# Squares of x: 64 products with ones on TensorE in place of 15 additions on VectorE

## The chip, the cores and the metric

One core of a Trainium2 chip runs the whole program. The metric is the time of one execution on the device in microseconds (us). The core's engines run side by side, each with its own queue in program order: TensorE (PE in the profile, its weight loads PEld), VectorE (DVE), ScalarE (ACT), GpSimd (POOL) and SyncE (SP), which issues the DMA transfers. They wait for one another by semaphores.

## The reference

Two layers of an encoder trunk over x, 512 positions of 2048 features, in float32. Each layer normalises x, scales and shifts it by values that come from a conditioning vector c, and mixes it. The start of it is what this case is about:

```python
def rms_norm(x, g):
    y = xf * lax.rsqrt(jnp.mean(xf * xf, axis=-1, keepdims=True) + EPS)
    return y * g

def ada_modulation(c, w_mod, b_mod):
    m = jax.nn.silu(c) @ w_mod + b_mod
    shift, scale, gate = jnp.split(m, 3, axis=-1)
    ...
for layer in range(DEPTH):
    shift, scale, gate = ada_modulation(c, w_mod[i], b_mod[i])
    h = rms_norm(x, norm_g[i]) * (1.0 + scale) + shift
    out = mixer(h, w_in[i], ..., w_out[i])
    x = x + gate * out
return rms_norm(x, final_norm_g)
```

The mixer of the first layer is an input projection 2048 to 8192 that feeds attention and a short convolution, and an output projection; that of the second is a gated unit with projections 2048 to 6144 and 2048 to 2048.

## The kernel before

x lies transposed: 16 tiles `x_t[kt]` of 128 features by 512 positions, loaded two tiles to a DMA, before everything else that is large. Since a position's features lie across partitions and across tiles, the mean of squares needs a sum over 16 tiles and then a sum over 128 partitions. The lines are those of the kernel before.

The head of the first layer goes like this. ScalarE squares the 16 tiles (L608). VectorE adds them up in two strands (L612) and the two strands together (L613, held as `total`). `inverse` (L201) sums over partitions: for each of four blocks of 128 positions one product with the block of squares as the stationary operand and one column of ones moving (L207), accumulated over the list of tiles that it is given; here that list has one tile. VectorE scales the four results into `r4` (L210, the tile is `r` in the profile), GpSimd raises them to -0.5 (L211). `rms` puts them on a diagonal (L218), `spread` multiplies that by ones (L224) and ScalarE copies the result to `r0` (L225), which holds the inverse root for each position on all partitions.

Beside this, `spread_cb` (L236) spreads silu(c) over all partitions into `cb` by 16 products (L241), whose results ScalarE and VectorE copy out. Conditioning is done on VectorE: `mod_tile` (L250) loads two halves of 128x1024 weights into `mraw` buffers and reduces each against `cb` with one instruction (L255, CUSTOM_DVE or ISA in the listings). In this stage there are five `mraw` buffers, and SyncE's queue waits at a load whose buffer has not been read.

The loop over the 16 tiles (L655) then does, per tile, two `mod_tile` (four halves: scale, then shift), `mod_scale` (L262), the loads of the projection weights and their split into a high and a low part (ScalarE L626, GpSimd L627), `modulated` (VectorE L562 into `tmp`, ScalarE L566 into `hh`, VectorE L569 into `lh`), and the products of the tile with the weights (L374 to L376). A scheduler sets the order on each engine from the order of the code and what depends on what; `tc.issue_after(total.ins)` tells it to place the first `mod_tile` of every round behind the last addition of squares.

The squares share their four group buffers (`hh`, four tiles each) with the high parts of the modulated tiles.

Of the kernel before, what the change touches and what calls it, by code (L numbers as in the profile page):

```python
# [11 lines left out]
AF = mybir.ActivationFunctionType  # L12
ALU = mybir.AluOpType
# [4 lines left out]
KT = D // P  # L18
# [97 lines left out]
def trunk(ctx, tc, xT, vecs, ab_wm, sg_wm, ab_wp, ab_wg, ab_wi, ab_wo, sg_wi, sg_wo, wsT, bs, rope, band, eye, out):  # L116
    nc = tc.nc
# [9 lines left out]
    def page(tag, bufs, dt=F32, pool=None):  # L127
        return (pool or work).tile([P, S], dt, tag=tag, bufs=bufs, name=tag)
# [44 lines left out]
    def bank():  # L173
        return psum.tile([P, S], F32, tag="ps", name="ps")
# [16 lines left out]
    x_t = Pages()  # L191
# [5 lines left out]
    def v1(c):  # L197
        return vec[:, c:c + 1]


    def inverse(parts, cols=ALL):  # L201
        n = (cols.stop - cols.start) // P
        sums = [bank() for _ in range(n)]
        for j, s in enumerate(parts):
            for i, acc in enumerate(sums):
                ts = slice(cols.start + i * P, cols.start + (i + 1) * P)
                nc.tensor.matmul(acc[:, 0:1], lhsT=s[:, ts], rhs=ones[:, 0:1], start=j == 0, stop=j == len(parts) - 1)  # L207
        r4 = const.tile([P, NT], F32, tag="r4", bufs=2, name="r4")
        for i, acc in enumerate(sums):
            nc.vector.tensor_scalar(out=r4[:, i:i + 1], in0=acc[:, 0:1], scalar1=1.0 / D, scalar2=EPS, op0=ALU.mult, op1=ALU.add)  # L210
        nc.gpsimd.tensor_tensor(out=r4[:, :n], in0=r4[:, :n], in1=mhalf[:, :n], op=ALU.pow)  # L211
        return r4

    def rms(parts, cols=ALL):
        r4, n = inverse(parts, cols), (cols.stop - cols.start) // P
        dg = page("tmp", 4)
        for i in range(n):
            nc.vector.tensor_scalar(out=dg[:, i * P:(i + 1) * P], in0=ident, scalar1=r4[:, i:i + 1], scalar2=None, op0=ALU.mult)  # L218
        return dg

    def spread(dg, r, cols=ALL):
        n = cols.stop - cols.start
        pr = bank()
        nc.tensor.matmul(pr[:, :n], lhsT=ones, rhs=dg[:, :n], start=True, stop=True)  # L224
        nc.scalar.copy(out=r[:, cols], in_=pr[:, :n])  # L225
# [24 lines left out]
    def mod_tile(pool, n, nt, bufs):  # L250
        src, b = wm[n]
        for h in range(2):
            raw = pool.tile([P, HALF], F32, tag="mraw", bufs=bufs, name="mraw")
            nc.sync.dma_start(out=raw, in_=src[nt, h])
            nc.vector.tensor_tensor_reduce(  # L255
                out=raw, in0=raw, in1=cb[:, h * HALF:(h + 1) * HALF], scale=0.5,
                scalar=v1(b + nt) if h == 0 else macc[n][:, nt:nt + 1], op0=ALU.mult, op1=ALU.add,
                accum_out=(mods if h else macc)[n][:, nt:nt + 1])

    def mod_scale(n, kt):  # L260
        g = v1((V_ABG if n == "ab" else V_SGG) + kt)
        nc.vector.scalar_tensor_tensor(  # L262
            out=gsc[n][:, kt:kt + 1], in0=mods[n][:, KT + kt:KT + kt + 1], scalar=1.0, in1=g,
            op0=ALU.add, op1=ALU.mult)
# [106 lines left out]
    def mm3(acc, w, m, first, last, **kw):  # L371


        nc.tensor.matmul(acc, lhsT=w[0], rhs=m[0], start=first, stop=False, **kw)  # L374
        nc.tensor.matmul(acc, lhsT=w[0], rhs=m[1], start=False, stop=False, **kw)  # L375
        nc.tensor.matmul(acc, lhsT=w[1], rhs=m[0], start=False, stop=last, **kw)  # L376

    class Pos:
# [3 lines left out]
        def slice(self):  # L382
            w = self.s.next(self.i, self.more)
            self.i += 1
            if self.tick:
                self.tick(self.s.last.ins)
            return w
# [171 lines left out]
    def modulated(n, kt, t, r, to, cols=ALL, keep=False):  # L559

        xr = page("tmp", 4)
        nc.vector.scalar_tensor_tensor(  # L562
            out=xr[:, cols], in0=t[:, cols], scalar=gsc[n][:, kt:kt + 1], in1=r[:, cols], op0=ALU.mult, op1=ALU.mult)
        hi, lo = to
        sh = mods[n][:, kt:kt + 1]
        nc.scalar.activation(out=hi[:, cols], in_=xr[:, cols], func=AF.Identity, bias=sh)  # L566
        if keep:
            nc.scalar.activation(out=t[:, cols], in_=xr[:, cols], func=AF.Identity, bias=sh)
        nc.vector.scalar_tensor_tensor(  # L569
            out=lo[:, cols], in0=xr[:, cols], scalar=sh, in1=hi[:, cols].bitcast(F32), op0=ALU.add, op1=ALU.subtract)  # L570
# [32 lines left out]
    pa = tc.alloc_tile_pool(name="pa", bufs=2, reuse_waits="tile")  # L603
    parts = []
    squares = Book("hh", F32)
    for kt in range(KT):
        sq = squares.page()
        nc.scalar.activation(out=sq, in_=x_t[kt], func=AF.Square)  # L608
        if kt < 2:
            parts.append(sq)  # L610
        else:
            nc.vector.tensor_tensor(out=parts[kt % 2], in0=parts[kt % 2], in1=sq, op=ALU.add)  # L612
    total = nc.vector.tensor_tensor(out=parts[0], in0=parts[0], in1=parts[1], op=ALU.add)  # L613
    r0 = page("R", 2)
    spread(rms(parts[:1]), r0)

# [1 line left out]
    def split_w(src, n, pool, bufs):  # L620
        raw = work.tile([P, HALF], F32, tag="wraw", bufs=3, name="wraw")[:, :n]
        size = HALF if pool is work else n
        hi = pool.tile([P, size], F32R, tag="whi", bufs=bufs, name="whi")[:, :n]
        lo = pool.tile([P, size], F32R, tag="wlo", bufs=bufs, name="wlo")[:, :n]
        nc.sync.dma_start(out=raw, in_=src)
        nc.scalar.copy(out=hi, in_=raw)  # L626
        nc.gpsimd.tensor_tensor(out=lo, in0=raw, in1=hi.bitcast(F32), op=ALU.subtract)  # L627
        return hi, lo
# [4 lines left out]
    def fetch(g, kts):  # L633
        for kt in kts:
            held[g, kt] = split_w(ab_wg[g, kt], S, pa, 8)

    def quarter(g, q):
        if q == 0:
            sums[g] = pa.tile([P, 4, S], F32, tag="sum", bufs=1, name="sum") if g == 1 else work.tile([P, 4, S], F32, tag="xy", bufs=4, name="xy")
        for f in range(4):  # L640
            acc = bank()
            cs = slice(f * P, (f + 1) * P)
            for i in range(4):
                kt = 4 * q + i
                (hi, lo), a = held[g, kt], h[kt]
                if g:
                    mm3(acc, (hi[:, cs], lo[:, cs]), a, i == 0, i == 3)
                else:
                    mm3(acc, (a[0][:, cs], a[1][:, cs]), (hi, lo), i == 0, i == 3)
            if q == 0:  # L650
                nc.scalar.copy(out=sums[g][:, f], in_=acc)
            else:
                nc.vector.tensor_tensor(out=sums[g][:, f], in0=acc, in1=sums[g][:, f], op=ALU.add)

    for kt in range(KT):  # L655
        with tc.issue_after(total.ins):
            mod_tile(pa, "ab", KT + kt, 5)
        mod_scale("ab", kt)
        mod_tile(pa, "ab", kt, 5)
        hi, lo = split_w(ab_wp[kt], W_P, work, 2)  # L660
        modulated("ab", kt, x_t[kt], r0, h.add())
        for f in range(6):
            cs = slice(f * P, (f + 1) * P)
            mm3(gates[f], (hi[:, cs], lo[:, cs]), h[kt], kt == 0, kt == KT - 1)
        fetch(0, [kt])
        q, i = divmod(kt, 4)
        if q:
            at = 4 * (q - 1) + 2 * (i % 2)
            fetch(1 + i // 2, [at, at + 1])
            if i % 2:  # L670
                quarter(1 + i // 2, q - 1)
        if i == 3:
            quarter(0, q)
# [211 lines left out]
    parts = right()  # L885
# [134 lines left out]
    parts = right()  # L1020
# [7 lines left out]
    for i in range(2):  # L1028
        for g in range(4):
# [5 lines left out]
            if g % 2:  # L1035
                (nc.scalar if g > 1 else nc.sync).dma_start(
                    out=out[1].rearrange("(t p n) -> t p n", t=2, p=P)[i, :, (g - 1) * S:(g + 1) * S].rearrange("p (g s) -> p g s", g=2),
                    in_=fin[i][:, g - 1:g + 1])
# [84 lines left out]
```

## Time and profile before

| | us |
|---|---|
| median of three runs | 1690.81 (1689.48 to 1692.96) |
| the profiled execution | 1690.71 |
| its span, first to last instruction | 1688.6 |
| TensorE busy | 1614.2 (96%) |
| VectorE busy | 1309.0 (78%) |
| ScalarE busy | 664.6 (39%) |
| GpSimd busy | 143.4 (8%) |

The shares are averages over the span. The chain that ended last, followed back from the end, is 80% TensorE and 13% VectorE. The page's 40 slices are 42 us each, with the busy share in tenths. The granted clock of TensorE is 1.00 at full speed (2.4 GHz) and 0.50 at its lower level (1.2 GHz).

### The profile page before, as it was taken

The numbers are of one execution on the slowest core, as the hardware profiler recorded it, in microseconds if no ns is written. First come the engines' busy times: TensorE is split into PE (matmuls) and PEld (weight loads), VectorE is DVE, ScalarE is ACT, GpSimd is POOL, SyncE is SP. The second block draws the span as 40 slices with busy tenths as digits, with TensorE's granted clock in tenths as the row PEclk, the third lists the DMA queues.
The fourth block names the chain that finished last, engine by engine and source line by source line (L and its number), as shares of the span: only waits on it lengthen the run. The fifth ranks groups of instructions, "written<-read, shape, count | busy, mean of one in ns | idle before, by whom it ended". The sixth has DMA issues, their size and how long they took to land.

```text
span 1688.6 us, 24674 instructions
## 1 busy us (share of the span) xinstructions
PE 1614.2 (96%) x9900; PEld 1440.9 (85%) x9900; DVE 1309.0 (78%) x1761; ACT 664.6 (39%) x953; POOL 143.4 (8%) x95
## 2 busy tenths in 40 slices
PE   5888999999999999999999999699999999999998
PEld 3676787888888888888889998699999999998998
DVE  7899748876766777766878876788998888898884
ACT  3232224332322332323544554344444444465552
POOL 2465521000000000000000000000000000000000
PEclk7999999999999999999999999799999999999999
DMA  8787544765666665764453432233333333235333
GB/s 312 255 278 261 193 129 144 225 227 193 225 210 232 216 224 182 247 210 164 135 190 125 152 130 69 75 101 101 100 101 101 103 100 118 97 101 199 109 99 115
DMA packets 85539, 276.44 MB, mean 164 GB/s; under 512 B 8753, under 2 KB 11057, under 8 KB 85425
## 3 DMA queue, kind: packets, MB, share of 16 engines
q1 hardware_dynamic: 85136, 273.82, 48.5%
q8 instruction: 77, 1.26, 0.3%
q10 hardware_dynamic: 288, 1.05, 0.2%
q14 instruction: 38, 0.30, 0.1%
HBM read 266.45 MB, written 8.39 MB: 163 GB/s over the span
## 4 chain that ended last, share of the span: by engine, by line
PE 80%; DVE 13%; issue 3%; ACT 2%; DMA 1%; SPq 0%; POOL 0%; POOLq 0%; DVEq 0%; ACTq 0%
PE ps L376 26%; PE ps L374 26%; PE ps L375 26%; DVE mraw L255 5%; DVE wlo L310 2%; ACT whi L309 1%; PE ps L974 1%; PE ps L735 1%; DVE gsc_ab L262 1%; DMA xy<-in_xT_dram 1%; DVE st L953 1%; DVE first L434 0%; ACT hh L566 0%; DVE lh L569 0%; DVE third L310 0%
## 5 line engine op out<-in xcount | busy, mean ns | idle before, releaser
L374 PE MATMUL ps<-hh,whi 128*128 128x512 f32 (+1 forms) x1600 | 568.3, 358 | 22.1 <-ACT hh L566 16.1
L376 PE MATMUL ps<-hh,wlo 128*128 128x512 f32 (+1 forms) x1600 | 566.5, 354 | 1.3 <-POOL wlo L627 1.3
L375 PE MATMUL ps<-lh,whi 128*128 128x512 f32 (+1 forms) x1600 | 566.3, 354 | 1.5 <-DVE lh L797 1.5
L374 PEld LDWEIGHTS ps<-hh,whi 128*128 128x128 f32 x1600 | 304.0, 190 | 68.8 <-ACT hh L566 19.8
L309 ACT CAST whi<-wraw 128x1024 fp32r<-128x1024 f32 x190 | 199.7, 1052 | 406.4 <-PE ps L375 294.2
L376 PEld LDWEIGHTS ps<-hh,wlo 128*128 128x128 f32 x1600 | 303.3, 190 | 44.1 <-POOL wlo L627 2.1
L375 PEld LDWEIGHTS ps<-lh,whi 128*128 128x128 f32 x1600 | 303.7, 190 | 43.5 <-DVE lh L797 1.9
L310 DVE TENSOR_TENSOR wlo<-wraw,whi 128x1024 fp32r<-128x1024 f32 x190 | 232.7, 1226 | 121.6 <-ACT whi L309 120.9
L255 DVE CUSTOM_DVE_ANT_0 mraw<-mraw,cb,vec 128x1024 f32<-128x1024 f32 x96 | 138.5, 1443 | 18.2 <-DMA mraw<-in_sg_wm_dram 12.9
L627 POOL TENSOR_TENSOR wlo<-wraw,whi 128x512 fp32r<-128x512 f32 (+1 forms) x64 | 114.9, 1814 | 105.8 <-ACT whi L626 93.0
L374 PE MATMUL ps<-whi,hh 128*128 128x512 f32 (+1 forms) x288 | 103.9, 361 | 19.5 <-ACT whi L309 15.1
L376 PE MATMUL ps<-sum,wlo 128*128 128x256 f32 x408 | 113.0, 277 | 0.9 <-DVE wlo L310 0.9
L374 PE MATMUL ps<-sum,whi 128*128 128x256 f32 x408 | 112.7, 276 | 0.0
L375 PE MATMUL ps<-sum,whi 128*128 128x256 f32 x408 | 112.7, 276 | 0.0
L309 ACT CAST whi<-first 128x1024 fp32r<-128x1024 f32 x56 | 58.8, 1050 | 116.4 <-DVE first L318 69.2
L375 PE MATMUL ps<-wlo,hh 128*128 128x512 f32 (+1 forms) x288 | 103.0, 358 | 0.8 <-DVE wlo L310 0.7
L376 PE MATMUL ps<-whi,lh 128*128 128x512 f32 (+1 forms) x288 | 102.8, 357 | 0.0
L310 DVE TENSOR_TENSOR wlo<-first,whi 128x1024 fp32r<-128x1024 f32 x56 | 68.4, 1222 | 26.2 <-ACT whi L309 26.2
L255 DVE CUSTOM_DVE_ANT_0 mraw<-mraw,cb,macc_ab 128x1024 f32<-128x1024 f32 x48 | 79.6, 1657 | 1.6 <-DMA mraw<-in_ab_wm_dram 0.5
L374 PEld LDWEIGHTS ps<-whi,hh 128*128 128x128 f32 x288 | 55.4, 192 | 29.5 <-ACT whi L309 15.5
L376 PEld LDWEIGHTS ps<-sum,wlo 128*128 128x128 f32 x408 | 76.6, 188 | 1.4 <-DVE wlo L310 1.4
L318 DVE TENSOR_TENSOR first<-first,wraw 128x1024 f32<-128x1024 f32 x63 | 76.8, 1219 | 0.5
(253 smaller groups left out, 2884.3 us busy)
## 6 DMA issues: line engine op xcount, KB each, us to landing
mraw<-in_ab_wm_dram SPq DMA_DIRECT2D x96, 512.0 KB, 4.6
mraw<-in_sg_wm_dram SPq DMA_DIRECT2D x96, 512.0 KB, 4.5
wraw<-in_ab_wi_dram SPq DMA_DIRECT2D x92, 512.0 KB, 3.6
wraw<-in_sg_wi_dram SPq DMA_DIRECT2D x75, 512.0 KB, 3.5
wraw<-in_ab_wo_dram SPq DMA_DIRECT2D x27, 512.0 KB, 3.5
wraw<-in_sg_wo_dram SPq DMA_DIRECT2D x27, 512.0 KB, 3.5
wraw<-in_ab_wg_dram SPq DMA_DIRECT2D x48, 256.0 KB, 2.8
first<-in_sg_wi_dram SPq DMA_DIRECT2D x21, 512.0 KB, 3.8
```

Of the source, the lines that this page charges most:

```text
L255: nc.vector.tensor_tensor_reduce(out=raw, in0=raw, in1=cb[:, h * HALF:(h + 1) * HALF], scale=0.5, scalar=v1(b + nt) if h == 0 else macc[n] ...
L262: nc.vector.scalar_tensor_tensor(out=gsc[n][:, kt:kt + 1], in0=mods[n][:, KT + kt:KT + kt + 1], scalar=1.0, in1=g, op0=ALU.add, op1=ALU.mult)
L309: nc.scalar.copy(out=hi, in_=raw)
L310: nc.vector.tensor_tensor(out=lo, in0=raw, in1=hi.bitcast(F32), op=ALU.subtract)
L318: nc.vector.tensor_tensor(out=r[a], in0=r[a], in1=r[b], op=ALU.add)
L374: nc.tensor.matmul(acc, lhsT=w[0], rhs=m[0], start=first, stop=False, **kw)
L375: nc.tensor.matmul(acc, lhsT=w[0], rhs=m[1], start=False, stop=False, **kw)
L376: nc.tensor.matmul(acc, lhsT=w[1], rhs=m[0], start=False, stop=last, **kw)
L627: nc.gpsimd.tensor_tensor(out=lo, in0=raw, in1=hi.bitcast(F32), op=ALU.subtract)
L735: nc.tensor.transpose(out=pt[:, i * P:(i + 1) * P], in_=ps[i][:, ks], identity=ident)
L953: nc.vector.bn_stats(out=st[:, j, n, :], in_=t)
L974: nc.tensor.matmul(accs[f][:, j * P:(j + 1) * P], lhsT=y.g[n][:, j, f * P:(f + 1) * P], rhs=wst[g // 4][:, g % 4 * P:(g % 4 + 1) * P], sta ...
```

## The change

All 16 squares are kept and handed to `rms`, so that the products with ones sum over tiles and partitions at once: 16 tiles by 4 blocks. Every fourth square is taken on VectorE instead of ScalarE. The additions go, and with them `total` and the `issue_after` that used it.

```diff
     for kt in range(KT):
         sq = squares.page()
-        nc.scalar.activation(out=sq, in_=x_t[kt], func=AF.Square)
-        if kt < 2:
-            parts.append(sq)
+        if kt % 4 == 3:
+            nc.vector.tensor_tensor(out=sq, in0=x_t[kt], in1=x_t[kt], op=ALU.mult)
         else:
-            nc.vector.tensor_tensor(out=parts[kt % 2], in0=parts[kt % 2], in1=sq, op=ALU.add)
-    total = nc.vector.tensor_tensor(out=parts[0], in0=parts[0], in1=parts[1], op=ALU.add)
+            nc.scalar.activation(out=sq, in_=x_t[kt], func=AF.Square)
+        parts.append(sq)
     r0 = page("R", 2)
-    spread(rms(parts[:1]), r0)
+    spread(rms(parts), r0)
...
     for kt in range(KT):
-        with tc.issue_after(total.ins):
-            mod_tile(pa, "ab", KT + kt, 5)
+        mod_tile(pa, "ab", KT + kt, 5)
         mod_scale("ab", kt)
```

The code above is what is written; the scheduler decides where each instruction stands. On VectorE, from the sum of squares to the first modulation of x (L562), the rows before are:

```order
L612 TENSOR_TENSOR hh<-hh 128x512 x10
L613 TENSOR_TENSOR hh<-hh 128x512
L255 ISA mraw,macc_ab<-mraw,cb,vec 128x1024
L255 ISA macc_ab 128x1
L210 TENSOR_SCALAR r_172<-ps 128x1 x4
L255 ISA mraw,mod_ab<-mraw,cb,macc_ab 128x1024
L255 ISA mod_ab 128x1
L218 TENSOR_SCALAR tmp<-ident,r_172 128x128 x4
L262 SCALAR_TENSOR_TENSOR gsc_ab<-mod_ab,vec 128x1
L255 ISA mraw,macc_ab<-mraw,cb,vec 128x1024
```

The same place in the changed kernel, whose line numbers are three smaller for the squares and up to two smaller further down:

```order
L609 TENSOR_TENSOR hh<-xy 128x512 x2
L210 TENSOR_SCALAR r_217<-ps 128x1 x4
L218 TENSOR_SCALAR tmp<-ident,r_217 128x128 x4
L255 ISA mraw,macc_ab<-mraw,cb,vec 128x1024
L255 ISA macc_ab 128x1
L255 ISA mraw,mod_ab<-mraw,cb,macc_ab 128x1024
L255 ISA mod_ab 128x1
L262 SCALAR_TENSOR_TENSOR gsc_ab<-mod_ab,vec 128x1
L255 ISA mraw,macc_ab<-mraw,cb,vec 128x1024
L255 ISA macc_ab 128x1
L562 SCALAR_TENSOR_TENSOR tmp<-xy,gsc_ab,R 128x512
```

The first two reductions (the rows with `cb`), which stood around the four `r` operations, stand behind the four of the diagonal. From the fourth reduction on the two orders run alike again.

On TensorE, before, from the products that spread silu(c) to the first products with weights:

```order
L241 MATMUL ps<-ident,cs 128x128 x16
L207 MATMUL ps<-ones,hh 128x1 x4
L224 MATMUL ps<-tmp,ones 128x512
L374 MATMUL ps<-hh,whi 128x512 x6
L374 MATMUL ps<-whi,hh 128x512
```

And in the changed kernel:

```order
L241 MATMUL ps<-ident,cs 128x128 x16
L207 MATMUL ps<-ones,hh 128x1 x64
L224 MATMUL ps<-tmp,ones 128x512
L374 MATMUL ps<-hh,whi 128x512
L375 MATMUL ps<-lh,whi 128x512
L376 MATMUL ps<-hh,wlo 128x512
```

Four products with ones have become 64, in the same place in the queue, in groups of four in the order of the tiles, each group waiting for its square.

## Rows read from the trace of the kernel before

**Rows 1.** The page's 40 slices: busy tenths of TensorE and VectorE.

```profile
PE   5888999999999999999999999699999999999998
DVE  7899748876766777766878876788998888898884
```

**Rows 2.** Busy time by stretch: us, busy time and count of each engine, granted clock.

```profile
core 0: us, PE busy (x) PEld busy (x) DVE busy (x) ACT busy (x) POOL busy (x), PEclk, DMA share, GB/s
9.30:11.00 1.70, 0.00 (x0) 0.00 (x0) 1.70 (x4) 1.70 (x4) 0.00 (x0) 1.00 1.06 412
11.00:11.50 0.50, 0.00 (x0) 0.00 (x0) 0.50 (x2) 0.50 (x2) 0.00 (x0) 0.81 1.02 393
...
18.60:20.60 2.00, 1.86 (x8) 1.78 (x8) 1.54 (x6) 0.00 (x0) 0.00 (x0) 0.50 1.04 415
...
28.40:184.00 155.60, 130.75 (x528) 102.19 (x528) 143.66 (x164) 43.90 (x70) 86.98 (x46) 0.96 0.76 264
184.00:260.00 76.00, 75.86 (x334) 62.63 (x335) 35.07 (x49) 21.04 (x33) 28.15 (x20) 1.00 0.43 139
```

**Rows 3.** Chain of waits, first 330 us: start, length, what ran.

```profile
14.77 1.16 ACT hh L608 x2
...
17.91 0.70 DVE hh L613
18.65 1.88 PE ps L207 x8
20.87 1.98 POOL r L211
...
23.89 2.06 PE ps L224 x2
...
26.59 0.75 DVE tmp L562
...
45.31 1.28 DVE mraw L255
46.64 1.28 DVE mraw L255
```

**Rows 4.** VectorE's waits, 28 to 185 us: total, times, longest.

```profile
DVE lh L569 <- ACT hh L566: 9.0, 12, 1.5
```

**Rows 5.** L612 and L608: ns min/median/max, first and last start, shapes.

```profile
L612 DVE TENSOR_TENSOR hh<-hh x14: 681/684/693, 7.8 to 17.2; 128x512 f32<-128x512 f32 x14
...
L608 ACT ACTIVATE hh<-xy x16: 612/621/635, 5.8 to 15.3; 128x512 f32<-128x512 f32 x16
```

**Rows 6.** L207, the products with ones, in the first 40 us.

```profile
L207 PE MATMUL ps<-ones,hh x8: 352/352/370, 18.7 to 20.2; 128*128 128x1 f32 x8
```

**Rows 7.** Weight loads in order of time around 980 us: start, length, instruction.

```profile
979.91 0.54 PEld L207 LDWEIGHTS ps<-ones,R 128*128 128x128 f32 x4
980.36 0.53 PEld L207 LDWEIGHTS ps<-ones,tmp 128*128 128x128 f32 x4
980.81 0.19 PEld L374 LDWEIGHTS ps<-hh,whi 128*128 128x128 f32 x1
```

**Rows 8.** L241, the products that spread silu(c).

```profile
L241 PE MATMUL ps<-ident,cs x32: 275/421/581, 3.2 to 9.0; 128*128 128x128 f32 x32
```

**Rows 9.** VectorE in order of time, 15 to 31 us.

```profile
18.52 1.28 DVE L255 CUSTOM_DVE_ANT_0 mraw<-mraw,cb,vec 128x1024 f32<-128x1024 f32 x1
...
20.68 1.28 DVE L255 CUSTOM_DVE_ANT_0 mraw<-mraw,cb,macc_ab 128x1024 f32<-128x1024 f32 x1
...
22.87 0.88 DVE L218 TENSOR_SCALAR tmp<-ident,r 128x128 f32<-128x128 f32 x4 [0.90 <-POOL r L211]
...
26.59 0.75 DVE L562 SCALAR_TENSOR_TENSOR tmp<-xy,gsc_ab,R 128x512 f32<-128x512 f32 x1 [0.25 <-ACT R L225]
```

**Rows 10.** VectorE's reductions by operands, 28 to 185 us: busy us, mean ns.

```profile
L255 DVE CUSTOM_DVE_ANT_0 mraw<-mraw,cb,macc_ab 128x1024 f32<-128x1024 f32 x28 | 52.6, 1879 | 0.8
L255 DVE CUSTOM_DVE_ANT_0 mraw<-mraw,cb,vec 128x1024 f32<-128x1024 f32 x28 | 47.8, 1705 | 1.3 <-DMA mraw<-in_ab_wm_dram 1.3
```

## The prediction

> **What bounds the kernel now.** I read the page's 40 slices first [rows 1]. TensorE is at 9 tenths or more from the fifth slice on; only the first four slices (42 us each) fall short, and there VectorE is at 7 to 9. A table by stretches sharpens this [rows 2]: from 28.4 to 184.0 us VectorE works 143.66 of 155.6 us, TensorE 130.75; from 184 to 260 TensorE works 75.86 of 76. So there are two regimes: a first stage paced by VectorE, then a stage paced by TensorE to the end. The change lies wholly at the head of the first stage.
>
> The chain of waits [rows 3] shows that head step by step. The last tiles of x are there at 14.77; ScalarE squares them until 15.9; VectorE's additions lag and end at 18.61 (17.91 + 0.70); four small products take 1.88 us; then come the power on GpSimd (1.98), the diagonal, the spreading product (2.06), the copy to r0 and at 26.59 the first modulation of x (L562). From there the chain is mostly conditioning reductions (L255) at a period of 1.33 us (46.64 - 45.31). In this stage VectorE waits little: 9.0 us, in 12 waits, for the ScalarE half of the modulation [rows 4]. A delay of VectorE's work at the head therefore finds no slack to vanish in: every later step of the stage hangs on it, and TensorE's stage behind that.
>
> **The change part by part.**
> *VectorE's work on squares.* Out go 15 additions of 0.684 us (10.3 us) [rows 5]; in come 4 squarings, a tensor_tensor on the same 128x512 shape, which I price alike (2.7 us). ScalarE loses 4 squares of 0.62 us. Neither is bounding any more: the last square, on VectorE, can start when x lands at 14.77 and ends near 15.5, against 18.61 for the sum now. If nothing else changed, that alone would be worth 3.1 us.
>
> *The products.* 4 become 64, each with a 128x128 block of squares as the stationary operand and one moving column. The row of L207 shows two passes per product (x8 for 4 products) [rows 6]. Cold, eight passes took 1.86 us, the last lasting about 0.36, so they start (1.86 - 0.36) / 7 = 0.214 us apart. Late in the kernel, where the clock is granted in full, the weight loads of eight such passes run from 979.91 to 980.81, 0.1125 us each [rows 7]. So 128 passes cost 14.3 us at the high clock (2.4 GHz) and 27.3 us at the low one (1.2 GHz). They are on the path: TensorE runs in order, and they stand behind the 32 passes of L241, whose last starts at 9.0 [rows 8]. A tile of x comes every 0.64 us (16 squares start between 5.8 and 15.3 [rows 5]), but four products need 0.9 us at best. TensorE is behind from its first product on and no longer waits for x.
>
> The Trainium skill, "TensorE: Matmul & The Clock Gate", section "LDWEIGHTS (loading the stationary operand)", prices a weight load by its columns alone, 128 / 1.2 = 107 ns: as an estimate, 128 loads would be 13.7 us at either clock. The rows agree at the high clock (0.1125) and not at the low one (0.214).
>
> *Which clock.* After L241 the granted clock stayed at 1.00 to 11.0 us, averaged 0.81 from 11.0 to 11.5 and was 0.50 by the time L207 ran [rows 2]: a mean of 0.81 is 0.31 us of the half microsecond at full clock, so it fell at 11.31, 2 us after TensorE's last pass. Now TensorE does not idle there, but what it does is load weights for single columns. No row shows a long run of that. Bounds: all at the high clock, the first pass starts one spacing after L241's last, at 9.11, and the last at 9.11 + 127 x 0.1125 = 23.4; falling at 11.31 as now, 2.20 / 0.1125 = 19.5 passes are done by then and 107.5 x 0.214 = 23.0 us follow, last start 34.3. Today's last pass starts at 18.65 + 1.50 = 20.15. The delay is 3.25 us by the first and 14.15 by the second. I take the second: the nearest row is L207's own, in the same place after the same L241, and it ran at 0.50 through all its passes.
>
> *Conditioning.* The issue_after goes, but the order on VectorE shows that the reductions do not come earlier. Now one pair of them runs between the sum and the diagonal, while TensorE and GpSimd work (18.52 and 20.68 [rows 9]); in the changed order both stand behind the four r4 operations (which wait for the last product) and the four of the diagonal (which wait for GpSimd). VectorE then idles from 15.5 until the last product, and its first reduction starts only after the diagonal. That moves two reductions out of cover: 2 x 1.33 = 2.66 us. The modulation waited 0.25 us for r0 [rows 9]; with two reductions more in front of it that wait is gone, so 2.4 us net. Queued behind the waiting r4 operations is everything VectorE does for the stage, and SP too: the reductions free the five mraw buffers, so loads beyond the fifth wait as well. That costs nothing of its own, because five tiles are there when VectorE starts, and it frees one per 1.33 us while it still has four to read.
>
> *After the head.* On SP and GpSimd the order of instructions stays as it was; ScalarE and TensorE differ beyond the squares only in a few rows of the first modulated tile, which wait for the same events. I price that at nothing, with an uncertainty: with GpSimd running, L255 averages 1.88 and 1.71 us over the stage [rows 10] instead of 1.28 [rows 9], 56 x 0.5 = 28 us in all. How the two engines mesh after a shifted start may move that by a tenth, 3 us either way.
>
> Sum: 14.15 + 2.4 = 16.55 us. The profiled execution took 1690.71 us (span 1688.6 and 2.1 around it), 0.1 below the median of the three runs, 1690.81. Forecast: 1690.7 + 16.6 = 1707.3 us, 1704 to 1711 on its own with the 3 us above.
>
> **Rivals.**
> 1. *The clock stays up.* A TensorE that is never idle keeps its 2.4 GHz through all 64 products. For it: the clock fell only after idling here. Against it: L207 ran wholly at 0.50. Time: 3.25 + 2.4 = 5.65 us, 1696.4 us (1693.4 to 1699.4). The Trainium skill, same page, section "What's actually happening", has the gate follow how busy the engine is; taken by its word, this rival would be the outcome. No run so far shows what a stream of one-column products counts for.
> 2. *Not slower: the products keep pace with x.* If weight loads slipped under one another, the products would follow each square, and the last pass would start near 15.6, just after the last square. The sum would be ready 4.5 us earlier than today, conditioning would give back 2.4, and the time would be 1690.7 - 2.1 = 1688.6 us. It decides from the point at which a product costs under 0.16 us (0.64 / 4); the cheapest pair of passes in the trace is 0.225. The Trainium skill, same page, section "Step-by-step: what each phase is for", speaks for it: the engine pulls the next load ahead of a running matmul. The rows already contain whatever of that happens.
> 3. *The change does not do what it says.* "Not queued behind" already fails in the order; that is in the sum. Were conditioning the part that counts and the products nearly free, it would be rival 2.
> 4. *Worse than forecast.* The clock falls at once and VectorE meshes badly with GpSimd: 27.3 us of products from 9.11, so 16.2 + 2.4 + 3 = 21.6, 1712 us.
>
> **How the numbers follow.** Forecast 0.57, rival 1 0.32, rival 2 (with 3) 0.07, rival 4 0.04. 0.2% is 3.4 us, about what a measurement of this kernel can tell from no change. Slower by more than that (over 1694.2) are the forecast, rival 4 and 0.27 of rival 1, whose low end lies under it: 0.88. Same gets the other 0.05 of rival 1 and 0.04 of rival 2, faster the remaining 0.03 of rival 2: 0.09 and 0.03. The range spans rival 1 and the forecast and leaves out rivals 2 and 4: 1693.5 to 1711; the forecast's own is 1704 to 1711.
>
> **What would show it.** In the changed profile, L207 should have 128 passes from about 9.1 with no gap, the last starting near 34 (forecast) or 23 (rival 1); the spacing changes from 0.11 to 0.21 where the granted clock goes to 0.50, near 11.3. VectorE should idle from about 15.5 until then, and its first L255 should follow the four L218. The diagonal now ends at 23.75 (22.87 + 0.88 [rows 9]); three reductions stand between it and L562, which should first start near 23.75 + 14.15 + 3 x 1.33 = 41.9 (forecast) or 31.0 (rival 1) instead of 26.59, and the stretch in which TensorE takes over should begin as much after 184 as the total grew. I am wrong if L207 ends before 20 us, if L255 runs before L210, or if the delay at L562 shrinks on the way to 184, which would mean slack in the first stage that I did not see.

## The result and the profile after

The changed kernel takes 1703.95 us (median of four runs, 1703.22 to 1705.17) against 1691.15 us before: a ratio of 1.0083 with a 95% interval of 1.0070 to 1.0096, 12.8 us or 0.8% slower. The profiled execution took 1703.22 us, its span is 1701.2.

The slices of the page show where: only the first one changes much. TensorE has 7 tenths there instead of 5, VectorE 3 instead of 7 [rows 1].

```profile
PE   7889899999999999999999999699999999999998
DVE  3889837867766767676878876688998888898884
```

By stretches (us, busy time and count of each engine, granted clock, share of the DMA engines, GB/s), to be held against [rows 2]:

```profile
core 0: us, PE busy (x) PEld busy (x) DVE busy (x) ACT busy (x) POOL busy (x), PEclk, DMA share, GB/s
9.30:11.00 1.70, 1.70 (x19) 1.70 (x17) 1.29 (x2) 1.33 (x3) 0.00 (x0) 1.00 1.05 407
11.00:11.50 0.50, 0.50 (x6) 0.50 (x7) 0.00 (x0) 0.50 (x2) 0.00 (x0) 1.00 1.07 410
11.50:15.00 3.50, 3.50 (x32) 3.50 (x31) 1.18 (x2) 2.57 (x5) 0.00 (x0) 0.95 1.06 417
15.00:18.00 3.00, 3.00 (x16) 3.00 (x16) 0.21 (x1) 0.15 (x1) 0.00 (x0) 0.50 1.03 418
24.00:27.00 3.00, 3.00 (x15) 3.00 (x16) 0.00 (x0) 0.00 (x0) 0.00 (x0) 0.50 0.00 0
```

TensorE works without a gap, and its clock falls all the same. A mean of 0.95 over 3.5 us is 3.15 us at full speed and the rest at half: it fell near 14.65, not at 11.31. In the stretch from 24 to 27 TensorE is the only thing that moves: VectorE has nothing it may do, and not a byte is loaded. The products as one group (ns min/median/max, first and last start), beside [rows 6]:

```profile
L207 PE MATMUL ps<-ones,hh x128: 169/352/353, 9.1 to 31.1; 128*128 128x1 f32 x128
```

128 passes, the last starting at 31.1, 10.95 us after the last one of before (20.15). VectorE in order of time, beside [rows 9]:

```profile
14.52 0.69 DVE L609 TENSOR_TENSOR hh<-xy 128x512 f32<-128x512 f32 x1 [1.83 <-DMA xy<-in_xT_dram]
30.19 0.16 DVE L210 TENSOR_SCALAR r<-ps 128x1 f32<-128x1 f32 x1 [14.98 <-PE ps L207]
...
32.83 0.87 DVE L218 TENSOR_SCALAR tmp<-ident,r 128x128 f32<-128x128 f32 x4 [1.20 <-POOL r L211]
33.62 1.28 DVE L255 CUSTOM_DVE_ANT_0 mraw<-mraw,cb,vec 128x1024 f32<-128x1024 f32 x1
...
35.04 1.28 DVE L255 CUSTOM_DVE_ANT_0 mraw<-mraw,cb,macc_ab 128x1024 f32<-128x1024 f32 x1
...
37.65 2.28 DVE L562 SCALAR_TENSOR_TENSOR tmp<-xy,gsc_ab,R 128x512 f32<-128x512 f32 x1
```

The row to read is the second: 14.98 us in which VectorE, the engine that paces this stage, waits for TensorE. Its first reduction comes at 33.62 instead of 18.52. SyncE waits with it: four loads of conditioning weights take 24.83 us to issue (11.86 in the kernel before; rows of SyncE's queue in order of time, the first before, the second after), because their buffers are not read.

```profile
13.51 11.86 SPq L254 DMA_DIRECT2D mraw<-in_ab_wm_dram  x4
```

```profile
13.26 24.83 SPq L254 DMA_DIRECT2D mraw<-in_ab_wm_dram  x4
```

Then the delay travels. The two reductions that the chain of waits had at 45.31 and 46.64 [rows 3] now stand here:

```profile
58.77 1.28 DVE mraw L255
60.09 1.28 DVE mraw L255
```

That is 13.46 us later. The first modulations of the 16 tiles, L562 as a group, run from 26.6 to 192.5 us before (first row) and from 37.6 to 205.2 after:

```profile
L562 DVE SCALAR_TENSOR_TENSOR tmp<-xy,gsc_ab,R x16: 741/752/1751, 26.6 to 192.5; 128x512 f32<-128x512 f32 x16
```

```profile
L562 DVE SCALAR_TENSOR_TENSOR tmp<-xy,gsc_ab,R x16: 750/752/2280, 37.6 to 205.2; 128x512 f32<-128x512 f32 x16
```

The last one is 12.7 us late, and the span is 12.6 us longer. Of 13.5 us at the head 0.8 were given back along the stage, none after it. In a second profile of the changed kernel (run 6) the third tile is as late and the last L562 starts at 204.0, so there 2.0 us were given back. What follows the stage hardly varies: in nine of the eleven profiles of this case the span ends 1495.8 to 1496.6 us after the start of the last L562 (1498.7 and 1498.2 in runs 3 and 8). How late the stage ends is, but for those two, what the kernel loses.

### The profile page after: what moved, and what is told of

It reads as the page before. It is cut to its first block, busy times and chain, and to the rows that moved or that the text cites. A ratio compares the mean times of both kernels' runs of the same rounds, so it can differ in the third digit from the quotient of the medians.

```text
span 1701.2 us, 24889 instructions
## 1 busy us (share of the span) xinstructions
PE 1636.1 (96%) x10020; PEld 1462.2 (86%) x10020; DVE 1299.7 (76%) x1750; ACT 663.5 (39%) x949; POOL 143.1 (8%) x95
## 4 chain that ended last, share of the span: by engine, by line
PE 79%; DVE 13%; issue 2%; ACT 2%; DMA 1%; DVEq 0%; POOLq 0%; ACTq 0%; SPq 0%
PE ps L376 26%; PE ps L374 26%; PE ps L375 26%; DVE mraw L255 4%; DVE wlo L310 2%; DMA mraw<-in_ab_wm_dram 1%; PE ps L972 1%; ACT whi L309 1%; PE ps L733 1%; DVE gsc_ab L262 1%; DVE tmp L562 1%; DVE st L951 1%; DVE first L434 0%; DVE third L310 0%; ACT hh L566 0%
## 5 line engine op out<-in xcount | busy, mean ns | idle before, releaser
L255 DVE CUSTOM_DVE_ANT_0 mraw<-mraw,cb,vec 128x1024 f32<-128x1024 f32 x96 | 137.6, 1434 | 22.9 <-DMA mraw<-in_sg_wm_dram 16.3
L310 DVE TENSOR_TENSOR wlo<-first,whi 128x1024 fp32r<-128x1024 f32 x56 | 68.4, 1222 | 26.6 <-ACT whi L309 26.6
L255 DVE CUSTOM_DVE_ANT_0 mraw<-mraw,cb,macc_ab 128x1024 f32<-128x1024 f32 x48 | 75.0, 1563 | 2.5 <-DMA mraw<-in_ab_wm_dram 1.5
```

What stands on the lines that cost most here:

```text
L255: nc.vector.tensor_tensor_reduce(out=raw, in0=raw, in1=cb[:, h * HALF:(h + 1) * HALF], scale=0.5, scalar=v1(b + nt) if h == 0 else macc[n] ...
L310: nc.vector.tensor_tensor(out=lo, in0=raw, in1=hi.bitcast(F32), op=ALU.subtract)
```

## The experiments

Each is compared with runs of the kernel before on the same chip; ratios are to those. "Reductions" are the conditioning instructions of L255, whose line moves by one to three in the variants. Eight kernels beside the changed one were run, in three sets.

**1. The order alone: reductions behind the diagonal, with the additions and 4 products of before.**

`last[0]` is the last instruction of the diagonal, kept by `rms`; the scale's `mod_tile` stands behind `total` already.

```diff
     spread(rms(parts[:1]), r0)
+    total = last[0]
...
-        mod_tile(pa, "ab", kt, 5)
+        with tc.issue_after(total.ins):
+            mod_tile(pa, "ab", kt, 5)
```

> The kernel before, with its additions and its 4 products, in which the scheduler is told to place the conditioning reductions behind the diagonal (L218), where the changed kernel has them. Theory A (two separate costs: the 64 products delay the sum of squares by 11 us, and two reductions moved out of the products' cover cost 2.4 us more): 1691.2 + 2.4 = 1693.6 us, with L562 first starting near 29.1 instead of 26.59. Rival B (the place of the reductions costs nothing, all of it is the products): 1691.2 us, within 0.05%.

Measured: ratio 1.0014 (1.0006 to 1.0023), 2.4 us on 1689.7, with an interval from 1.0 to 3.9. Its VectorE in order of time:

```profile
20.05 0.16 DVE L210 TENSOR_SCALAR r<-ps 128x1 f32<-128x1 f32 x1 [0.27 <-PE ps L207]
21.41 0.88 DVE L220 TENSOR_SCALAR tmp<-ident,r 128x128 f32<-128x128 f32 x4 [1.20 <-POOL r L211]
22.20 1.28 DVE L257 CUSTOM_DVE_ANT_0 mraw<-mraw,cb,vec 128x1024 f32<-128x1024 f32 x1
...
28.90 1.63 DVE L564 SCALAR_TENSOR_TENSOR tmp<-xy,gsc_ab,R 128x512 f32<-128x512 f32 x1
...
45.37 0.75 DVE L564 SCALAR_TENSOR_TENSOR tmp<-xy,gsc_ab,R 128x512 f32<-128x512 f32 x1
```

The first reduction comes at 22.20 instead of 18.52, the modulation at 28.90, near the expected 29.1. By the time, the place of the reductions has a price of its own, the smaller part of the 12.8 us; rival B, within 0.05%, lies just outside the interval.

The trace does not show that price at the head. The diagonal starts 1.46 us sooner than before (21.41 against 22.87), because the additions end 0.5 us sooner and GpSimd's power takes 1.02 us instead of 1.98. Four reductions then stand in a row, where the changed kernel has three. By the third tile (45.37, the last row) the modulation is only 0.73 us later than in the kernel before:

```profile
44.64 0.75 DVE L562 SCALAR_TENSOR_TENSOR tmp<-xy,gsc_ab,R 128x512 f32<-128x512 f32 x1
```

At the last tile it is 3.2 us later (195.7 against 192.5), in an execution that is the slowest of the eleven (1693.6). So 2.4 us is the price of this order as a whole; that it is the lost cover of two reductions is not shown.

**2. Two reductions ahead of the r4 operations in the changed kernel.**

```diff
-    spread(rms(parts), r0)
+    early = [mod_tile(pa, "ab", nt, 5) for nt in (KT, 0, KT + 1, 1)[:1]]
+    spread(rms(parts, behind=early[-1].ins), r0)
...
```

`behind` makes the r4 operations follow the last of the early reductions, and the loop leaves out what is already there.

> The changed kernel, in which the first two reductions are placed ahead of the r4 operations, under the products. Theory A: 1704.0 - 2.7 = 1701.3 us; the products still end near 31 and L562 starts near 36, when r0 is there. Rival B: unchanged, 1704 us. Rival C (the price is VectorE's idle time, not the lateness of r0): also 2.7 us less, so this run does not part A and C.

Measured: ratio 1.0079 (1.0062 to 1.0097), 1702.85 us, with runs from 1698.6 to 1707.2. That does not part 1701.3 from 1704. The profiled run shows a new loss: the diagonal took 3.43 us instead of 0.87, beside GpSimd. It does not explain why the median is no lower, for this execution is the fastest of the six (1698.6), and in it the third tile is modulated 3.8 us sooner than in the changed kernel (54.27 against 58.10). Why the six spread so far stays open.

```profile
33.66 3.43 DVE L219 TENSOR_SCALAR tmp<-ident,r 128x128 f32<-128x128 f32 x4 [0.90 <-POOL r L212]
```

**3. Eight reductions ahead.** The same edit with `[:4]`.

> The changed kernel with the first eight reductions ahead of the r4 operations, so that VectorE works through most of the time in which TensorE makes the products. Theory A (r0 is late by 11 us whatever VectorE does meanwhile): as with two ahead, 1701.3 us. Rival C (the stage is paced by VectorE's work alone, so what it gets done in the gap comes back in full): eight reductions at 1.33 us, 1704.0 - 10.6 = 1693.4 us.

Measured: ratio 1.0037 (1.0026 to 1.0049), 1695.6 us: by the two ratios 0.46% or 8 us less than the changed kernel, where theory A has 2.7 and rival C 10.6. The intervals of the two ratios leave 4.8 to 10.7 us, which shuts out A and just holds C. The products were as slow as ever (the last pass at 31.0, the stretch from 15 to 30 wholly TensorE's at half clock), but VectorE worked 10.57 us of that stretch instead of 0.21:

```profile
15.00:30.00 15.00, 15.00 (x72) 15.00 (x72) 10.57 (x19) 1.93 (x4) 0.00 (x0) 0.50 0.95 353
```

By the medians a quarter of C's gain is missing. In the traces the last first modulation starts 10.1 us sooner than in the changed kernel (195.1 against 205.2), but the span is only 7.4 us shorter: 2.7 us are lost behind the stage, and why stays open. Again the diagonal was slow, now 5.00 us, while GpSimd split weights beside it (VectorE's row, then GpSimd's):

```profile
32.73 5.00 DVE L219 TENSOR_SCALAR tmp<-ident,r 128x128 f32<-128x128 f32 x4 [1.20 <-POOL r L212]
```

```profile
32.66 4.79 POOL L629 TENSOR_TENSOR wlo<-wraw,whi 128x768 fp32r<-128x768 f32 x3
```

So r0 came later still than in the changed kernel (the first modulation starts at 40.56 against 37.65), and the kernel was faster by 8 us. Theory A's word, that a late r0 costs what it is late, falls; rival C is much the nearer: the price is, in the main, the time in which VectorE does nothing.

**4. All 128 columns in each product.**

```diff
+        m = P if len(parts) == KT else 1
-                nc.tensor.matmul(acc[:, 0:1], lhsT=s[:, ts], rhs=ones[:, 0:1], ...)
+                nc.tensor.matmul(acc[:, :m], lhsT=s[:, ts], rhs=ones[:, :m], ...)
...
```

The part left out places both `mod_tile` of every round behind the diagonal.

> The changed kernel, in which each of the 64 products moves all 128 columns of ones instead of one (the 128 result columns are equal and the first is used), with the reductions kept behind the diagonal. A pass is still as long as its weight load. Theory A with the clock as the term: TensorE stays at 2.4 GHz, passes are 0.11 us apart to the end, the last starts near 23.5 instead of 31.1, and the time falls by 7.6 us to 1696.4 us. Rival D (the passes are slow for another reason than the clock): 0.21 us apart in the second half as before, 1704 us or more.

Measured: ratio 1.0011 (1.0001 to 1.0021), 1691.6 us. The clock stayed up, and the passes stayed short to the last (a stretch, and the products as a group):

```profile
15.00:23.00 8.00, 8.00 (x74) 8.00 (x73) 0.20 (x2) 1.37 (x3) 0.41 (x1) 1.00 0.99 398
```

```profile
L208 PE MATMUL ps<-ones,hh x128: 275/275/275, 9.1 to 23.3; 128*128 128x128 f32 x128
```

128 times the columns, and the last pass starts at 23.3 instead of 31.1. Rival D falls. But the kernel got 12.4 us faster, not 7.6. The constraint that kept the reductions behind the diagonal had also let the scheduler put four reductions in a row and issue loads in another order, so this is not the products alone.

**5. 64 columns, in the order of the changed kernel.** The edit of 4 with `m = 64` and no constraint on the reductions.

> The changed kernel, in which each of the 64 products moves 64 columns of ones instead of one. The order on every engine stays that of the changed kernel but for three swaps on VectorE, the largest a reduction that comes ahead of the last r4 operation and the diagonal. If the clock alone is the term and 64 columns keep it up: the last pass near 23.4, 7.6 us less for it and up to 1.3 us for the reduction, 1703.9 - 7.6 to 8.9 = 1695 to 1696.3 us, above the run with 128 columns (1691.6), whose surplus then belongs to the other order that the scheduler gave it. If that surplus came from the products too: 1691.6 us. If 64 columns don't keep the clock: 1704 us.

Measured: ratio 1.0030 (1.0020 to 1.0041), 1694.5 us. The clock stayed at 1.00, the last pass started at 23.6, one reduction ran ahead of the diagonal:

```profile
15.00:23.00 8.00, 8.00 (x74) 8.00 (x74) 0.12 (x1) 0.06 (x1) 0.00 (x0) 1.00 0.86 348
```

```profile
23.84 1.28 DVE L256 CUSTOM_DVE_ANT_0 mraw<-mraw,cb,vec 128x1024 f32<-128x1024 f32 x1
...
26.40 0.88 DVE L219 TENSOR_SCALAR tmp<-ident,r 128x128 f32<-128x128 f32 x4 [1.20 <-POOL r L212]
```

This is the cleaner run on the clock: 10.3 us less than the changed kernel in the same set (1704.85, below), where the products and the reduction were to give 7.6 to 8.9. The intervals of the two ratios leave 6.7 to 12.9 us, so the expectation lies inside. The traces give it more closely: the third tile is modulated at 50.15 (row), 7.95 us sooner than in the changed kernel (58.10 in both of its profiles).

```profile
50.15 0.75 DVE L563 SCALAR_TENSOR_TENSOR tmp<-xy,gsc_ab,R 128x512 f32<-128x512 f32 x1
```

The clock was up in both runs and the last pass nearly as early, so the surplus of run 4 over this one, 2.9 us, most likely goes with the other order; what in it does so stays open.

**6. The changed kernel once more, in the same set.**

> The changed kernel itself on this chip, beside the others. Theory: 1704 us, 0.8% above the kernel before, with the clock falling between 13.5 and 15 us, later than the 11.3 to 11.7 of the kernels that add on VectorE. Against it: if the instant of the fall is a matter of chance from run to run, it may lie anywhere from 11.3 up, and the time between 1700 and 1707.

Measured: ratio 1.0088 (1.0073 to 1.0103), 1704.85 us. The clock fell near 13.68 (0.84 between 13 and 14), with TensorE busy throughout:

```profile
13.00:14.00 1.00, 1.00 (x10) 1.00 (x9) 0.00 (x0) 0.68 (x2) 0.00 (x0) 0.84 1.08 424
14.00:30.00 16.00, 16.00 (x77) 16.00 (x77) 0.69 (x1) 1.10 (x2) 0.00 (x0) 0.50 0.50 201
```

In the four profiles with 64 one-column products the fall lies between 13.7 and 14.7, after first passes at 8.7 to 9.1; in the two with 15 additions and 4 products it lies at 11.3 (before) and 11.7 (run 1).

**7. 128 columns and six reductions ahead.** Runs 4 and 2 together, with `[:3]` and no other constraint.

> The 64 products with 128 columns, and the first six conditioning reductions placed ahead of the r4 operations, so that VectorE has work from 16 to 24 us. If VectorE's lost time sets the price (theory C): VectorE's first reduction starts near 16 instead of 18.52, its idle time at the head is 2 to 3 us, and the time is that of the kernel before less 1 to 4 us, 1686 to 1689. If the lateness of r0 sets it (theory A): r0 comes near 29 instead of 26.6, 1692 to 1694 us.

Measured: ratio 0.9989 (0.9980 to 0.9998), 1687.5 us against 1689.8, 2.3 us faster than the kernel before, although r0 is later than there: the modulation starts at 32.49 instead of 26.59.

```profile
15.83 1.28 DVE L257 CUSTOM_DVE_ANT_0 mraw<-mraw,cb,vec 128x1024 f32<-128x1024 f32 x1 [0.71 <-DMA mraw<-in_ab_wm_dram]
...
23.46 1.28 DVE L257 CUSTOM_DVE_ANT_0 mraw<-mraw,cb,macc_ab 128x1024 f32<-128x1024 f32 x1
...
26.22 3.42 DVE L220 TENSOR_SCALAR tmp<-ident,r 128x128 f32<-128x128 f32 x4 [1.14 <-POOL r L213]
...
32.49 1.42 DVE L565 SCALAR_TENSOR_TENSOR tmp<-xy,gsc_ab,R 128x512 f32<-128x512 f32 x2 [0.31 <-ACT R L227]
```

VectorE reduces from 15.83 on, as soon as weights land, and ends the sixth reduction at 24.74, half a microsecond after the last product. The time is theory C's, and outside A's range.

**8. Pairs: half the additions, half the products.**

```diff
-        if kt % 4 == 3:
+        if kt == KT - 1:
             nc.vector.tensor_tensor(out=sq, in0=x_t[kt], in1=x_t[kt], op=ALU.mult)
...
-        parts.append(sq)
+        if kt % 2:
+            nc.vector.tensor_tensor(out=parts[-1], in0=parts[-1], in1=sq, op=ALU.add)
+        else:
+            parts.append(sq)
```

> VectorE adds the squares of each pair of tiles (8 additions of 15), the last square is VectorE's, and TensorE sums the 8 pairs by 32 products with 128 columns. Four products need 0.9 us and a pair of tiles of x comes every 1.29 us, so TensorE keeps pace with x: the last pass near 17, r0 some 3 us sooner than in the kernel before, the first reduction near 16.5 instead of 18.5. Theory C: 2 us less than before, 1688 us. If the head of the stage is bound by something else, such as the landing of the conditioning weights: no change, 1690 us.

Measured: ratio 0.9990 (0.9981 to 0.9999), 1688.5 us, 1.3 us faster than before. TensorE kept pace with x (the 64 passes, then VectorE):

```profile
L208 PE MATMUL ps<-ones,hh x64: 275/275/377, 8.7 to 17.6; 128*128 128x128 f32 x64
```

```profile
16.53 1.28 DVE L256 CUSTOM_DVE_ANT_0 mraw<-mraw,cb,vec 128x1024 f32<-128x1024 f32 x1
...
23.91 0.75 DVE L563 SCALAR_TENSOR_TENSOR tmp<-xy,gsc_ab,R 128x512 f32<-128x512 f32 x1 [0.25 <-ACT R L226]
```

The sum, the first reduction and r0 come 2 to 3 us sooner, as expected. The time follows by 1.3 us, with an interval from 0.2 to 3.2. The trace is that of the slowest of the eleven executions (1692.6): in it the third tile is 2.2 us sooner than before (42.46 against 44.64), the last one only 0.2 (192.3 against 192.5), so there the lead did not last through the stage, and behind it 2 us more are lost.

**9. Run 7 with GpSimd's first splits behind the copy to r0.**

```diff
-        nc.scalar.copy(out=hi, in_=raw)
+        with tc.issue_after(behind) if behind else nullcontext():
+            nc.scalar.copy(out=hi, in_=raw)
...
```

`behind` is the copy to r0, for the two splits of tile 0.

> The run with 128 columns and six reductions ahead, in which ScalarE's first two casts of weights are placed behind the copy to r0, so that GpSimd does not split weights while VectorE makes the diagonal. Beside GpSimd the diagonal took 3.42 us there, alone it takes 0.87. If that is a loss on the path: the diagonal 0.87, r0 2.5 us sooner, and the time 2.5 us under the 1687.5 of that run, 1685 us, 0.25% under the kernel before. If GpSimd's work only moves to collide with VectorE later: no change, 1687.5 us.

Measured: ratio 0.9980 (0.9969 to 0.9991), 1688.1 us against 1690.85, the largest gain over the kernel before of all runs, 0.2%. Whether it is better than run 7 the intervals don't say. The diagonal is short again, and the collision has moved: the modulations behind it now take 2.96 for two, which alone are 0.75 each, beside GpSimd (VectorE's rows, then GpSimd's).

```profile
26.18 0.87 DVE L220 TENSOR_SCALAR tmp<-ident,r 128x128 f32<-128x128 f32 x4 [1.13 <-POOL r L213]
...
29.50 2.96 DVE L565 SCALAR_TENSOR_TENSOR tmp<-xy,gsc_ab,R 128x512 f32<-128x512 f32 x2
```

```profile
29.73 8.33 POOL L631 TENSOR_TENSOR wlo<-wraw,whi 128x768 fp32r<-128x768 f32 x4 [3.58 <-ACT whi L630]
```

## Why the prediction was right

*The products on the path:* right, and the term was too large. The passes cost what [rows 6, 7] gave for either clock, without a gap from 9.1 on. The size failed at one step, "falling at 11.31 as now": it fell near 14.65. By the prediction's own sum, (14.65 - 9.1) / 0.1125 = 49 passes are done by then and 78 x 0.214 = 16.7 us follow, a last start of 31.3; measured 31.1. The delay is 10.95 us instead of 14.15, and that is nearly the whole distance between 1707.3 and 1703.95. The measured time lies just below the forecast's own range (1704 to 1711), inside the wider one.

*Which clock:* the choice between the ends was right: it fell. Rival 1 would have had it stay at 2.4 GHz; runs 4 and 5, in which it did stay, show that rival's last pass (23.3 and 23.6 against 23.4), reached by more columns and not by being busy. The trace had no row for a long stream of single columns, so that the clock would fall was a choice by the nearest row, which came out; when it would fall no row told. The mechanism of the delay was reasoned; that the time came so near the low-clock end was in part luck. The Trainium skill, "TensorE: Matmul & The Clock Gate", section "What's actually happening", lets the gate follow how busy the engine is; where the profile's busy time is taken for that, this trace does not agree, with 3.00 of 3.00 us busy at a clock of 0.50.

*The reductions moved out of cover:* the sum fits, in part by luck. The third tile is 13.46 us late, against 10.95 + 2.4 = 13.35. But two things in it were not foreseen and nearly cancel: GpSimd's power took 1.02 us instead of 1.98, and the first L562 took 2.28 us instead of 0.75, beside GpSimd. Nor do the orders run alike from the fourth reduction on: it stands ahead of the first modulation before (25.05 against 26.59) and behind it after (39.85 against 37.65), so that one reduction more, not two, delays the first modulation, which is 11.06 us late. Run 1 measured 2.4 us for an order much like this one, but its trace has only 0.73 of it at the third tile. So the term is not shown by itself.

*After the head, nothing:* nearly right. 0.8 us of 13.5 came back along the stage, 2.0 in the second profile, both inside the 3 us allowed for how VectorE and GpSimd mesh.

*Rivals 2 to 4:* TensorE did not keep pace with x (0.9 us and more for four products against 0.64), as run 8 confirms from the other side, where it has 1.29 us for four and does keep pace. The fall came later, not at once, so rival 4 did not come either.

What the prediction said too simply is why the delay costs anything. It let the lateness of the sum be the price. In run 3 the first modulation comes 3 us later than in the changed kernel, in run 7 6 us later than in the kernel before, and each is the faster of the two; in both VectorE has reductions to do meanwhile. By these runs the delay of the products and the place of the reductions are one loss: VectorE's idle time at the head, 15 us in a row. In the same stretch of the kernel before (row, columns as in [rows 2]) VectorE works 13.30 us of 14.98, on the last additions up to 18.6 and then on five reductions, the diagonal and the first modulation.

```profile
15.21:30.19 14.98, 5.62 (x14) 3.70 (x15) 13.30 (x27) 3.65 (x7) 4.79 (x3) 0.50 0.83 312
```

## What to carry to other kernels

Work that is taken off the pacing engine gains nothing if that engine then waits for the result; look at what its queue may do meanwhile, and put independent work ahead of the first instruction that waits. Price a small product by its weight load at both clocks, not by its moving columns, and compare four of them with the rate at which their inputs arrive. Where a sum can be shared, as in the pairs, size the share so that neither engine falls behind the loads.

## What the runs showed of the hardware

- A stream of products with one moving column did not hold TensorE's clock: in four profiles it fell to 1.2 GHz 5.0 to 5.5 us after the stream's first pass, with no gap in the engine's work. With 64 or 128 columns in the same stream it stayed at 2.4 GHz to the last pass (runs 4 and 5). A pass took 0.112 us in all three at the high clock, 0.214 at the low one, so the added columns cost nothing.
- A diagonal of four tensor_scalar operations (128x128) took 0.87 us alone and 3.42, 3.43 and 5.00 us beside GpSimd's splits (runs 7, 2 and 3). The Trainium skill, "SBUF — State Buffer", section "Who interferes with whom", says that such operations can take a port pair that VectorE shares with GpSimd, and that the one that comes second waits for the whole instruction; the rows agree: in run 3 the diagonal lasted 4.13 us longer beside 4.79 us of GpSimd's work.
- GpSimd's power on four columns took 1.98 us in the kernel before [rows 3], where a reduction ran on VectorE, and 1.02 in the changed one, where VectorE idled (GpSimd in order of time):

```profile
31.78 1.02 POOL L211 TENSOR_TENSOR r<-r,mhalf 128x4 f32<-128x4 f32 x1 [30.91 <-DVE r L210]
```
